# A quarter turn of an 8192 x 8192 matrix: six of eight output columns turned by VectorE and ScalarE instead of TensorE

## The chip, the core and the metric

The kernel runs on one core of a Trainium2 chip. The metric is the time of one execution in microseconds (us), as the device reports it, median of the runs; the launch on the host is not in it. A profiled execution of the same kernel gives the span from the first to the last instruction and the busy times of the engines: TensorE (PE for its products, PEld for its weight loads), VectorE (DVE), ScalarE (ACT), GpSimd (POOL) and SyncE (SP), and of the 16 DMA engines that move data between HBM and the on-chip memories SBUF and PSUM, both of 128 partitions.

## The reference

```python
def setup_inputs():
    return {"x": np.random.randn(8192, 8192).astype(np.float32), "k": 1}

def reference(x, k):
    return np.rot90(x, k)
```

With k = 1 element (r, c) of x goes to row 8191 - c, column r of the output: a transpose, with the columns of x taken from the last to the first. Nothing is computed; 268.4 MB are read and 268.4 MB written.

## The kernel before

**Tiling.** x is cut into 16 macro tiles of 1024 rows by 4096 columns (`macros`, index `kk`). A macro tile comes in as 8 loads (`t` = 0 to 7, T = 8) of 128 rows by 4096 columns, 2 MiB each, one row a partition; load number `m` is `kk * 8 + t`. It goes out as 8 outputs (`j` = 0 to 7, J = 8), each made of the 512 columns of one `j` over all 1024 rows: 512 output rows in 4 groups of 128 partitions, 1024 elements a row, 2 MiB. The last macro tile is put out otherwise: in two halves of 4 loads (END), two `j` at a time, in rows of 512 elements. One of its outputs is split in two (`n_few`): a quarter, put out with 64 partitions by 16 small stores from SyncE, and three quarters by one store.

**Buffers.** Five buffers of 2 MiB (`bufs`): in steady state two take loads (LAND) and three hold outputs (OUTS). Between them lies `ring`, 63 slots of 128 x 512 elements; slot numbers come from `slot(kk, t, j)`, and a macro tile's load `t` lands in the slots that output `t` of the macro tile before has left. So load m = n + 8 can be put into the ring only when output n has been read out of it.

**The work of the engines.** They run side by side, each through its own list in program order, and wait on semaphores.

- SyncE issues the loads (L178). From the sixth on each waits until VectorE has emptied the buffer (`s_rev`).
- VectorE (L238 to L256) waits for the load, waits for the slots, and copies the 8 x 512 columns into the ring with the order in each 512 reversed (L248). A load is cut into two or three pieces, by which slots are free first.
- TensorE (L268 to L293) turns 128 x 128 blocks: 32 transposes (L279) an output, 16 for each half of PSUM (`ps[0]`, `ps[1]`). Of output 0 of a macro tile the blocks of early loads are turned as they land.
- ScalarE (L299 to L331) waits for room in an out buffer (the store three outputs back), copies each half of PSUM into it (L317, 128 x 2048), and issues the store (L326).

`s_half` counts turned halves, `s_ev` evicted ones, `s_store` and `s_land` finished DMAs.

Of the kernel before, what the change touches and what calls it, by code (L numbers as in the profile page):

```python
# [6 lines left out]
P = 128  # L7
# [3 lines left out]
T = R // P  # L11
W = 4096
G = 4
J = W // (G * P)
# [3 lines left out]
CH = G * P  # L18
F = G * R
SLOTS = T * J - 1  # L20

END = T // 2

H = 2
LAND = 2
OUTS = 3

FEW = 16
LEFT = 4
# [23 lines left out]
def slot(kk, t, j):  # L53

    at = t * J + j if kk % 2 == 0 else J + t + j * T
    return (at + kk // 2 * (J + 1)) % SLOTS


def kernel(tc: tile.TileContext, x: bass.AP, k: bass.AP, out: bass.AP):
# [19 lines left out]
    n_few = n_out - J + 2  # L79
    kk, ts, js = outs[n_few]  # L80
    assert len(js) == 2 and END * P * H * G == F
    blocks = [(j, g * P, P) for j in reversed(js) for g in range(G)]
    few = [[(js[-1], g * P // 2 + h * FEW, P // 2) for g in range(G)] for h in range(H)]
    outs[n_few] = (kk, ts, js, few)
    outs.insert(n_few + 1, (kk, ts, js, [blocks[2 : 2 + G], blocks[2 + G :]]))
    n_out += 1

    def halves(n):
        if len(outs[n]) == 4:
            return outs[n][3]  # L90
        blocks = [(j, g * P, P) for j in reversed(outs[n][2]) for g in range(G)]
        return [blocks[: len(blocks) // H], blocks[len(blocks) // H :]]


    order = [(kk, a, b) for kk in range(KK) for a in range(T) for b in range(J)]
    for i, (kk, t, j) in enumerate(order):
        if i >= SLOTS:
            pk, pj, pt = order[i - SLOTS]
            assert slot(kk, t, j) == slot(pk, pt, pj)

    with tc.tile_critical():  # L101
# [9 lines left out]
        ]  # L111

# [4 lines left out]
        s_first = nc.alloc_semaphore("s_first")  # L117
        s_half = nc.alloc_semaphore("s_half")
        s_ev = nc.alloc_semaphore("s_ev")
        s_few = nc.alloc_semaphore("s_few")  # L120
# [14 lines left out]

        pieces, rev = {}, {}
        done = 0
        for m in range(n_load):  # L140
            kk, t = divmod(m, T)
            got = []
            if m >= T:
                full = (s_half, H * (m - T + 1))
                first = (s_first, m - T + 2)
            else:
                full = None
                first = (s_first, 1) if t == T - 1 else None
            begin = wide if kk == KK - 1 else 1
            cuts = [0, begin, J - 1, J] if t == T - 1 else [0, J - 1, J]  # L150
            if m < T - 1:
                cuts = [0, J]
            for lo, hi in zip(cuts[:-1], cuts[1:]):
                got.append((lo, hi, first if hi == J else full if lo == 0 else None))
                done += 1
                for j in range(lo, hi):
                    rev[m, j] = done
            pieces[m] = got

        def runs(kk, t, lo, hi):  # L160

            at = [slot(kk, t, j) for j in range(lo, hi)]
            i = 0
            while i < len(at):
                n = 1
                step = at[i + 1] - at[i] if i + 1 < len(at) else 1
                if step > 0:
                    while i + n < len(at) and at[i + n] - at[i + n - 1] == step:
                        n += 1
                else:  # L170
                    step = 1
                yield lo + i, n, at[i], step
                i += n
# [14 lines left out]
        with nc.Block() as block:  # L188
# [15 lines left out]
            @block.sync  # L204
            def _(e):
                for m in range(LAND + OUTS, n_load):
                    last = [i for i in range(m) if load_buf(i) == load_buf(m)]
                    e.wait_ge(s_rev, rev[last[-1], J - 1])
                    load(e, m)
                kk, ts, js, _ = outs[n_few]  # L210
                b = out_buf(n_few)
                top = M - macros[kk][1] - (js[-1] + 1) * CH
                left = macros[kk][0] + ts[0] * P
                rows = len(ts) * P
                for h in range(H):
# [14 lines left out]
                e.wait_ge(s_few, 16 * 2 * H * LEFT)  # L230
                for b in range(LAND + OUTS):
                    n = sum(out_buf(i) == b and i != n_few for i in range(n_out))
                    if n:
                        e.wait_ge(s_store[b], 16 * n)

            @block.vector
            def _(e):
                for m in range(n_load):  # L238
                    kk, t = divmod(m, T)
                    b = load_buf(m)  # L240
                    a = bufs[b][:].rearrange("p (j c) -> p j c", c=CH)
                    e.wait_ge(s_land[b], 16 * (uses_before(m, load_buf) + 1))
                    for lo, hi, wait in pieces[m]:
                        if wait:
                            e.wait_ge(*wait)
                        for j, n, at, step in runs(kk, t, lo, hi):
                            v = ring[:, at * CH : (at + (n - 1) * step + 1) * CH]
                            i = e.tensor_copy(  # L248
                                out=bass.AP(
                                    tensor=v.tensor,  # L250
                                    offset=v.offset,
                                    ap=[v.ap[0], [step * CH, n], [1, CH]],
                                ),
                                in_=a[:, j : j + n, ::-1],
                            )
                        i.then_inc(s_rev, 1)  # L256

            @block.tensor
            def _(e):
# [8 lines left out]
                for n, (kk, ts, js, *_) in enumerate(outs):  # L268
                    parts = halves(n)
                    rows = len(ts) * P  # L270

                    def transpose(t, h, b):
                        j, off, width = parts[h][b]
                        if n:
                            wait(s_ev, H * (n - 1) + h + 1)
                        wait(s_rev, rev[kk * T + t, j])
                        at = slot(kk, t, j) * CH + off
                        f = b * rows + (t - ts[0]) * P
                        i = e.transpose(  # L279
                            ps[h][:width, f : f + P], ring[:, at : at + width], ident  # L280
                        )
# [12 lines left out]

            @block.scalar
            def _(e):
                e.wait_ge(s_id, 2)
                e.copy(scratch, ident[:, :1])  # L298
                for n, (kk, ts, js, *_) in enumerate(outs):  # L299
                    r0, c0 = macros[kk]  # L300
                    parts = halves(n)
                    rows = len(ts) * P
                    b = out_buf(n)
                    for h in range(H):
                        if h == 0:
# [11 lines left out]
                        e.copy(  # L317
                            bufs[b][:width, h * F // H : h * F // H + f], ps[h][:width, :f]
                        ).then_inc(s_ev, 1)
                    if n == n_few:  # L320
                        continue
# [45 lines left out]
```

## Time and profile before

| | |
|---|---|
| median of 3 runs | 1264.5 us (1264.1 to 1264.59) |
| profiled execution, its own time | 1264.36 us |
| its span, first to last instruction | 1262.3 us |
| PE busy / PEld busy | 726.8 us (58%) / 683.2 us (54%), 4120 transposes |
| DVE busy | 403.0 us (32%), 313 instructions |
| ACT busy | 469.7 us (37%), 260 instructions |
| DMA | 537.48 MB, mean 426 GB/s |
| loads: 128 of 2048 KB | 16.8 us from issue to landing (median) |
| stores: 127 of 2048 KB, one of 1536 KB, 16 of 32 KB | 25.6 us for the large ones (median) |

Busy shares are of the span. The DMA row counts every byte that the engines moved, instructions included. The time from issue to landing holds the time that a transfer spends behind others in its queue.

### The profile page before, as it was taken

What the parts mean: (1) busy time and instruction counts of PE and PEld (TensorE: products, weight loads), DVE (VectorE), ACT (ScalarE), POOL (GpSimd) and SP (SyncE); (2) the same over time, 40 slices, a digit from 0 to 9 for tenths busy, and PEclk for the clock granted to TensorE, in tenths of its full rate; (3) what the DMA queues carried; (4) which work ended last, traced back from release to release, by engine and by line L of the source; (5) the groups of instructions that cost most, each with busy time, mean ns of one, the idle gap of its engine ahead of it and who ended that gap; (6) DMA issues with size and microseconds to landing.
All of it is one profiled execution on the core that took longest, in us unless ns stands there. A gap on an engine that the chain in (4) does not pass through costs nothing.

```text
span 1262.3 us, 9427 instructions
## 1 busy us (share of the span) xinstructions
PE 726.8 (58%) x4120; PEld 683.2 (54%) x4120; DVE 403.0 (32%) x313; ACT 469.7 (37%) x260; POOL 0.7 (0%) x6
## 2 busy tenths in 40 slices
PE   1566566665546645566555655566555655556564
PEld 1456465665545545565554655555555654556564
DVE  3323432324323343322342233422234222442210
ACT  0343333433334333433334333343333433434364
POOL 0000000000000000000000000000000000000000
PEclk9967767676787777777777776777777777777888
DMA  9999999999999999999999999999999999999998
GB/s 399 416 430 430 428 428 429 428 430 429 428 429 428 429 429 430 427 429 432 427 428 430 430 428 428 431 429 427 430 429 428 429 429 428 430 430 428 429 412 361
DMA packets 37032, 537.48 MB, mean 426 GB/s; under 512 B 4160, under 2 KB 4160, under 8 KB 4160
## 3 DMA queue, kind: packets, MB, share of 16 engines
q10 hardware_dynamic: 18432, 267.92, 50.0%
q1 hardware_dynamic: 18560, 268.97, 49.9%
q8 instruction: 32, 0.52, 0.2%
q14 instruction: 8, 0.07, 0.0%
HBM read 268.44 MB, written 268.44 MB: 425 GB/s over the span
## 4 chain that ended last, share of the span: by engine, by line
DMA 80%; issue 8%; DVE 5%; ACT 4%; PE 1%; SPq 1%; ACTq 0%
DMA buf<-in_x_dram 70%; DMA out_dram<-buf 11%; DVE ring L248 5%; ACT buf L317 4%; PE ps L279 1%; SPq L220 1%; ACTq L326 0%; SPq L178 0%; ACTq L314 0%; SPq L362 0%; SPq L101 0%
## 5 line engine op out<-in xcount | busy, mean ns | idle before, releaser
L279 PE MATMUL ps<-head,ring 128*128 128x128 f32 x4120 | 726.8, 357 | 522.7 <-ACT buf L317 462.3
L279 PEld LDWEIGHTS ps<-head,ring 128*128 128x128 f32 x4120 | 683.2, 190 | 566.1 <-ACT buf L317 497.2
L317 ACT COPY buf<-ps 128x2048 f32<-128x2048 f32 (+1 forms) x258 | 468.3, 1867 | 781.1 <-DMA out_dram<-buf 609.3
L248 DVE COPY ring<-buf 128x512 f32<-128x512 f32 (+7 forms) x313 | 403.0, 1337 | 811.4 <-DMA buf<-in_x_dram 810.1
L298 ACT ACT_TABLE_LOAD x1 | 1.3, 1283 | 0.9 <-SPq L101 0.9
L194 POOL TENSOR_SCALAR_AFFINE_SELECT head<-head 128x128 f32<-128x128 f32 x1 | 0.3, 292 | 0.2 <-POOL head L192 0.2
L192 POOL MEMSET head<- 128x128 f32 x1 | 0.2, 205 | 0.5 <-SPq L101 0.5
L298 ACT COPY head<-head 128x1 f32<-128x1 f32 x1 | 0.2, 191 | 0.0
L348 POOL MEMSET const-bfloat16-1.0<- 128x1 bf16 x1 | 0.1, 101 | 0.0
L348 POOL MEMSET const-uint8-127<- 128x1 uint8 x1 | 0.1, 101 | 0.0
L348 POOL MEMSET const-float32-0.0<- 128x1 f32 x1 | 0.1, 100 | 0.2 <-issue 0.2
L348 POOL MEMSET const-float32-1.0<- 128x1 f32 x1 | 0.1, 98 | 0.0
## 6 DMA issues: line engine op xcount, KB each, us to landing
buf<-in_x_dram SPq DMA_DIRECT2D x128, 2048.0 KB, 16.8
out_dram<-buf ACTq DMA_DIRECT2D x127, 2048.0 KB, 25.6
out_dram<-buf ACTq DMA_DIRECT2D x1, 1536.0 KB, 9.8
out_dram<-buf SPq DMA_DIRECT2D x16, 32.0 KB
```

The costliest lines, as they stand in the source:

```text
L192: e.memset(ident, 0.0).then_inc(s_id, 1)
L194: e.affine_select(out=ident, in_=ident, compare_op=mybir.AluOpType.not_equal, fill=1.0, base=0, pattern=[[-1, P]], channel_multiplier=1,). ...
L220: e.dma_start(out=bass.AP(tensor=out.tensor, offset=out[first : first + 1, left : left + 1].offset, ap=[[LEFT * M, FEW // LEFT], [4 * FEW ...
L248: i = e.tensor_copy(out=bass.AP(tensor=v.tensor, offset=v.offset, ap=[v.ap[0], [step * CH, n], [1, CH]],), in_=a[:, j : j + n, ::-1],)
L279: i = e.transpose(ps[h][:width, f : f + P], ring[:, at : at + width], ident)
L298: e.copy(scratch, ident[:, :1])
L317: e.copy(bufs[b][:width, h * F // H : h * F // H + f], ps[h][:width, :f]).then_inc(s_ev, 1)
L348: nc = _bacc.Bacc("TRN2", target_bir_lowering=False, num_devices=1)
```

## The change

The outputs of macro tiles 0 to 14 are divided (`in_quadrants`): `j` = 0 and 4 (BY_PE) are turned by TensorE as before, the other six by VectorE and ScalarE. For these six, VectorE puts the load's columns into the ring by 32 x 32 transposes (`e.transpose`, L289) in place of the reversing copy; 90 outputs in all. What is then left is to move whole 32 x 32 blocks from one group of 32 partitions to another (`moves`): 16 copies an output, each of 32 partitions by 8 x 4 x 32 elements, 8 of them by VectorE (L276) and 8 by ScalarE (L344), straight from the ring to the out buffer.

VectorE's list changes with it. Before it waits for load m = n + 8 it does its copies of output n, for which it waits for room in the out buffer (`room_for`) and for the macro tile's last load; and before it writes load m into the ring it waits for ScalarE's copies (`s_act`) and for its own (`s_dve`). ScalarE issues the store of such an output when both counts are there.

The ring becomes a fixed grid of 8 x 8 chunks, of which 63 lie in SBUF; the 64th, of load 7 and output 7, lies in the last 512 columns of PSUM (`corner`, in `ps[1]`). It makes 16 copies more for output 7, out of PSUM. So an output of TensorE is cut into three parts of 2048, 1536 and 512 columns (`parts`), the third in `ps[0]` again, and the last macro tile's transposes, which use all of PSUM, wait for all copies of the moved outputs (L306 to L308). A load is cut into two pieces (`j` 0 and 4, and the rest), load 7 of a macro tile into five. The last macro tile's outputs are 8 of 2 MiB; the split one and its 16 small stores go.

```diff
+Q = 32
+BY_DVE = 8
+BY_PE = [0, 4]
+
 END = T // 2
 
 H = 2
 LAND = 2
 OUTS = 3
-
-FEW = 16
-LEFT = 4
...
-    at = t * J + j if kk % 2 == 0 else J + t + j * T
-    return (at + kk // 2 * (J + 1)) % SLOTS
+    return t * J + j if kk % 2 == 0 else j * J + t
...
-    n_few = n_out - J + 2
-    kk, ts, js = outs[n_few]
-    assert len(js) == 2 and END * P * H * G == F
-    blocks = [(j, g * P, P) for j in reversed(js) for g in range(G)]
-    few = [[(js[-1], g * P // 2 + h * FEW, P // 2) for g in range(G)] for h in range(H)]
-    outs[n_few] = (kk, ts, js, few)
-    outs.insert(n_few + 1, (kk, ts, js, [blocks[2 : 2 + G], blocks[2 + G :]]))
-    n_out += 1
...
+    outs = [(*o, [(j, g * P) for j in reversed(o[2]) for g in range(G)]) for o in outs]
+    def in_quadrants(kk, j):
+        return kk < KK - 1 and j not in BY_PE
+
+    moved = [in_quadrants(kk, js[0]) for kk, _, js, _ in outs]
+
+
+    parts, seen = {}, 0
+    for n, (kk, ts, js, blocks) in enumerate(outs):
+        if moved[n]:
+            continue
+        end = len(blocks) * len(ts) * P
+        ends = [F // H, F - CH, F] if kk < KK - 1 else [F // H, end]
+        parts[n] = []
+        for i, (lo, hi) in enumerate(zip([0, *ends], ends)):
+            parts[n].append((seen, i % H, lo, hi))
+            seen += 1
+
+    def moved_until(n):
+        return sum(moved[: n + 1])
...
+        corner = ps[1][:, F // H - CH :]
...
+        def room_for(e, n):
+            b = out_buf(n)
+            stores = [i for i in range(n) if out_buf(i) == b]
+            loads = [i for i in range(n_load) if load_buf(i) == b]
+            if stores:
+                e.wait_ge(s_store[b], 16 * len(stores))
+            elif loads:
+                e.wait_ge(s_rev, rev[loads[-1], J - 1])
...
+            by_pe = list(range(J)) if kk == KK - 1 else BY_PE
+            rest = [j for j in range(J) if j not in by_pe]
+            if t < T - 1:
+                got = [js for js in (by_pe, rest) if js]
             else:
-                full = None
-                first = (s_first, 1) if t == T - 1 else None
-            begin = wide if kk == KK - 1 else 1
-            cuts = [0, begin, J - 1, J] if t == T - 1 else [0, J - 1, J]
-            if m < T - 1:
-                cuts = [0, J]
-            for lo, hi in zip(cuts[:-1], cuts[1:]):
-                got.append((lo, hi, first if hi == J else full if lo == 0 else None))
+                if kk == KK - 1:
+                    got = [by_pe[:wide], by_pe[wide:-1], by_pe[-1:]]
+                else:
+                    got = [by_pe[:1], *neighbours(rest[:-1]), by_pe[1:], rest[-1:]]
+            assert sorted(j for js in got for j in js) == list(range(J))
...
+        def moves(n, share):
+            kk, ts, (j,), _ = outs[n]
+            rows = len(ts) * P
+            cut = T - 1 if j == J - 1 else T
+            s, ((step, _),) = spaced([slot(kk, t, j) for t in ts[:cut]])
+            for lo, hi, v, first in ((0, cut, ring[:], s * CH), (cut, T, corner, 0)):
+                for a, q in share if lo < hi else []:
+                    yield (
+                        at(
+                            bufs[out_buf(n)][q * Q : q * Q + Q, :],
+                            lo * P + a * Q,
+                            [[P, hi - lo], [rows, G], [1, Q]],
+                        ),
+                        at(
+                            v[a * Q : a * Q + Q, :],
+                            first + q * Q,
+                            [[step * CH, hi - lo], [P, G], [1, Q]],
+                        ),
+                    )
+
+        pairs = [(a, q) for a in range(P // Q) for q in range(P // Q)]
...
-                kk, ts, js, _ = outs[n_few]
-                b = out_buf(n_few)
-                top = M - macros[kk][1] - (js[-1] + 1) * CH
-                left = macros[kk][0] + ts[0] * P
-                rows = len(ts) * P
-                for h in range(H):
-                    e.wait_ge(s_ev, H * n_few + h + 1)
-                    for at in (0, 2 * FEW):
-                        for d in range(LEFT):
-                            first = top + h * FEW + at + d
-                            e.dma_start(
-                                out=bass.AP(
-                                    tensor=out.tensor,
-                                    offset=out[first : first + 1, left : left + 1].offset,
-                                    ap=[[LEFT * M, FEW // LEFT], [4 * FEW * M, G], [1, rows]],
-                                ),
-                                in_=bufs[b][
-                                    at + d : at + FEW : LEFT, h * F // H : (h + 1) * F // H
-                                ].rearrange("m (g f) -> m g f", f=rows),
-                            ).then_inc(s_few, 16)
-                e.wait_ge(s_few, 16 * 2 * H * LEFT)
                 for b in range(LAND + OUTS):
...
                 for m in range(n_load):
                     kk, t = divmod(m, T)
                     b = load_buf(m)
-                    a = bufs[b][:].rearrange("p (j c) -> p j c", c=CH)
+                    n = m - T
+                    if n >= 0 and moved[n]:
+                        room_for(e, n)
+                        e.wait_ge(s_rev, rev[n // J * T + T - 1, n % J])
+                        for to, of in moves(n, pairs[:BY_DVE]):
+                            i = e.tensor_copy(out=to, in_=of)
+                        i.then_inc(s_dve, 1)
                     e.wait_ge(s_land[b], 16 * (uses_before(m, load_buf) + 1))
-                    for lo, hi, wait in pieces[m]:
-                        if wait:
-                            e.wait_ge(*wait)
-                        for j, n, at, step in runs(kk, t, lo, hi):
-                            v = ring[:, at * CH : (at + (n - 1) * step + 1) * CH]
-                            i = e.tensor_copy(
-                                out=bass.AP(
-                                    tensor=v.tensor,
-                                    offset=v.offset,
-                                    ap=[v.ap[0], [step * CH, n], [1, CH]],
-                                ),
-                                in_=a[:, j : j + n, ::-1],
-                            )
-                        i.then_inc(s_rev, 1)
+                    if n >= 0:
+                        if moved[n]:
+                            e.wait_ge(s_dve, moved_until(n))
+                            e.wait_ge(s_act, moved_until(n))
+                        else:
+                            e.wait_ge(s_half, turned_until(n))
+                    for js in pieces[m]:
+                        if (m, js[0]) == (n_load - 1, J - 1):
+                            e.wait_ge(s_half, turned_until(KK * J - J))
+                        turn = e.transpose if in_quadrants(kk, js[0]) else e.tensor_copy
+                        turn(out=chunk(kk, t, js), in_=landed(b, js)).then_inc(s_rev, 1)
 
             @block.tensor
             def _(e):
@@ -265,64 +298,61 @@
                         e.wait_ge(sem, n)
 
                 e.wait_ge(s_id, 2)
-                for n, (kk, ts, js, *_) in enumerate(outs):
-                    parts = halves(n)
+                used = {}
+                for n, (kk, ts, js, blocks) in enumerate(outs):
+                    if moved[n]:
+                        continue
                     rows = len(ts) * P
-
-                    def transpose(t, h, b):
-                        j, off, width = parts[h][b]
-                        if n:
-                            wait(s_ev, H * (n - 1) + h + 1)
+                    if n == KK * J - J:
+                        wait(s_act, moved_until(n))
+                        wait(s_dve, moved_until(n))
+                    order = [
+                        (part, f) for part in parts[n] for f in range(part[2], part[3], P)
+                    ]
+                    if js[0] == 0 and kk < KK - 1:
+                        late = parts[n][-1]
+                        order.sort(key=lambda o: (o[0] == late, o[1] % rows, o[1]))
+                    last = dict(order)
+                    for part, f in order:
+                        _, h, lo, _ = part
+                        j, off = blocks[f // rows]
+                        t = ts[f % rows // P]
+                        if used.get(h, part) != part:
+                            wait(s_ev, used[h][0] + 1)
                         wait(s_rev, rev[kk * T + t, j])
-                        at = slot(kk, t, j) * CH + off
-                        f = b * rows + (t - ts[0]) * P
                         i = e.transpose(
-                            ps[h][:width, f : f + P], ring[:, at : at + width], ident
+                            ps[h][:, f - lo : f - lo + P],
+                            chunk(kk, t, [j])[:, 0, off : off + P],
+                            ident,
                         )
-                        if t == ts[-1] and b == len(parts[h]) - 1:
+                        if f == last[part]:
                             i.then_inc(s_half, 1)
-                        elif t == ts[0] and h == H - 1 and b == len(parts[h]) - 1:
-                            i.then_inc(s_first, 1)
-
-                    order = [
-                        (t, h, b) for h in range(H) for b in range(len(parts[h])) for t in ts
-                    ]
-                    if js[0] == 0:
-                        order.sort()
-                    for t, h, b in order:
-                        transpose(t, h, b)
+                            used[h] = part
 
             @block.scalar
             def _(e):
                 e.wait_ge(s_id, 2)
                 e.copy(scratch, ident[:, :1])
-                for n, (kk, ts, js, *_) in enumerate(outs):
+                for n, (kk, ts, js, blocks) in enumerate(outs):
                     r0, c0 = macros[kk]
-                    parts = halves(n)
                     rows = len(ts) * P
                     b = out_buf(n)
-                    for h in range(H):
-                        if h == 0:
-                            stores = [i for i in range(n) if out_buf(i) == b]
-                            loads = [i for i in range(n_load) if load_buf(i) == b]
-                            if stores and stores[-1] == n_few:
-                                e.wait_ge(s_few, 16 * 2 * H * LEFT)
-                            elif stores:
-                                e.wait_ge(s_store[b], 16 * sum(i != n_few for i in stores))
-                            elif loads:
-                                e.wait_ge(s_rev, rev[loads[-1], J - 1])
-                        e.wait_ge(s_half, H * n + h + 1)
-                        width = parts[h][0][2]
-                        f = len(parts[h]) * rows
-                        e.copy(
-                            bufs[b][:width, h * F // H : h * F // H + f], ps[h][:width, :f]
-                        ).then_inc(s_ev, 1)
-                    if n == n_few:
-                        continue
-                    groups = sum(len(part) for part in parts)
+                    room_for(e, n)
+                    if moved[n]:
+                        e.wait_ge(s_rev, rev[kk * T + T - 1, js[0]])
+                        for to, of in moves(n, pairs[BY_DVE:]):
+                            i = e.copy(to, of)
+                        i.then_inc(s_act, 1)
+                        e.wait_ge(s_act, moved_until(n))
+                        e.wait_ge(s_dve, moved_until(n))
+                    else:
+                        for k, h, lo, hi in parts[n]:
+                            e.wait_ge(s_half, k + 1)
+                            e.copy(bufs[b][:, lo:hi], ps[h][:, : hi - lo]).then_inc(s_ev, 1)
+                        e.wait_ge(s_ev, turned_until(n))
+                    groups = len(blocks)
                     top = M - c0 - js[0] * CH - groups * P
                     left = r0 + ts[0] * P
-                    e.wait_ge(s_ev, H * (n + 1))
                     e.dma_start(
                         out=out[top : top + groups * P, left : left + rows].rearrange(
                             "(g m) f -> m g f", m=P

```

More of the change, by code (lines that the diff above doesn't have):

```diff
@@ L78, with turned_until @@
     assert len(outs) == n_out
-    n_few = n_out - J + 2
-    kk, ts, js = outs[n_few]
-    assert len(js) == 2 and END * P * H * G == F
-    blocks = [(j, g * P, P) for j in reversed(js) for g in range(G)]
-    few = [[(js[-1], g * P // 2 + h * FEW, P // 2) for g in range(G)] for h in range(H)]
-    outs[n_few] = (kk, ts, js, few)
-    outs.insert(n_few + 1, (kk, ts, js, [blocks[2 : 2 + G], blocks[2 + G :]]))
-    n_out += 1
[L88 to L99, printed above, removed]
+    outs = [(*o, [(j, g * P) for j in reversed(o[2]) for g in range(G)]) for o in outs]
[14 more added lines that the diff above has]
+        return sum(moved[: n + 1])
+    def turned_until(n):
+        return sum(len(parts[i]) for i in range(n + 1) if i in parts)
     with tc.tile_critical():
@@ L116 @@
         s_rev = nc.alloc_semaphore("s_rev")
-        s_first = nc.alloc_semaphore("s_first")
         s_half = nc.alloc_semaphore("s_half")
         s_ev = nc.alloc_semaphore("s_ev")
-        s_few = nc.alloc_semaphore("s_few")
+        s_dve = nc.alloc_semaphore("s_dve")
+        s_act = nc.alloc_semaphore("s_act")
         def load_buf(m):
@@ L134, in out_buf, with neighbours @@
             return ends[e % len(ends)]
+        def room_for(e, n):
[6 more added lines that the diff above has]
+                e.wait_ge(s_rev, rev[loads[-1], J - 1])
+        def neighbours(js):
+            cuts = [i for i in range(1, len(js)) if js[i] != js[i - 1] + 1]
+            return [js[lo:hi] for lo, hi in zip([0, *cuts], [*cuts, len(js)])]
         pieces, rev = {}, {}
@@ L141 @@
             kk, t = divmod(m, T)
[L142 to L145, printed above, removed]
-            else:
-                full = None
-                first = (s_first, 1) if t == T - 1 else None
-            begin = wide if kk == KK - 1 else 1
-            cuts = [0, begin, J - 1, J] if t == T - 1 else [0, J - 1, J]
-            if m < T - 1:
-                cuts = [0, J]
-            for lo, hi in zip(cuts[:-1], cuts[1:]):
-                got.append((lo, hi, first if hi == J else full if lo == 0 else None))
+            by_pe = list(range(J)) if kk == KK - 1 else BY_PE
@@ new lines @@
+            rest = [j for j in range(J) if j not in by_pe]
+            if t < T - 1:
+                got = [js for js in (by_pe, rest) if js]
+            else:
+                if kk == KK - 1:
[3 more added lines that the diff above has]
+            assert sorted(j for js in got for j in js) == list(range(J))
+            pieces[m] = got
+            for js in got:
@@ L155, with spaced @@
                 done += 1
-                for j in range(lo, hi):
+                for j in js:
                     rev[m, j] = done
[L158 to L173, printed above, removed]
+        def spaced(js):
+            step = js[1] - js[0] if len(js) > 1 else 1
+            n = 1
+            while n < len(js) and js[n] - js[n - 1] == step:
+                n += 1
+            if n == len(js):
+                return js[0], [[step, n]]
+            far = js[n] - js[0]
+            assert js == [js[0] + i * far + s * step for i in range(len(js) // n) for s in range(n)]
+            return js[0], [[far, len(js) // n], [step, n]]
@@ new lines, in at, with landed, chunk @@
+        def at(v, first, dims):
+            return bass.AP(
+                tensor=v.tensor, offset=v[:, first : first + 1].offset, ap=[v.ap[0], *dims]
+            )
+        def landed(b, js):
+            j, dims = spaced(js)
+            return at(
+                bufs[b][:], (j + 1) * CH - 1, [*([s * CH, n] for s, n in dims), [-1, CH]]
+            )
+        def chunk(kk, t, js):
+            if (t, js[0]) == (T - 1, J - 1):
+                if kk < KK - 1:
+                    return at(corner, 0, [[CH, 1], [1, CH]])
+                return at(ring[:], 0, [[CH, 1], [1, CH]])
+            s, dims = spaced([slot(kk, t, j) for j in js])
+            assert max(slot(kk, t, j) for j in js) < SLOTS
+            return at(ring[:], s * CH, [*([d * CH, n] for d, n in dims), [1, CH]])
@@ new lines, in moves @@
+        def moves(n, share):
[16 more added lines that the diff above has]
+                        ),
+                    )
@@ L209, in _ @@
                     load(e, m)
-                kk, ts, js, _ = outs[n_few]
-                b = out_buf(n_few)
-                top = M - macros[kk][1] - (js[-1] + 1) * CH
-                left = macros[kk][0] + ts[0] * P
-                rows = len(ts) * P
-                for h in range(H):
-                    e.wait_ge(s_ev, H * n_few + h + 1)
-                    for at in (0, 2 * FEW):
-                        for d in range(LEFT):
-                            first = top + h * FEW + at + d
-                            e.dma_start(
-                                out=bass.AP(
-                                    tensor=out.tensor,
-                                    offset=out[first : first + 1, left : left + 1].offset,
-                                    ap=[[LEFT * M, FEW // LEFT], [4 * FEW * M, G], [1, rows]],
-                                ),
-                                in_=bufs[b][
-                                    at + d : at + FEW : LEFT, h * F // H : (h + 1) * F // H
-                                ].rearrange("m (g f) -> m g f", f=rows),
-                            ).then_inc(s_few, 16)
-                e.wait_ge(s_few, 16 * 2 * H * LEFT)
                 for b in range(LAND + OUTS):
-                    n = sum(out_buf(i) == b and i != n_few for i in range(n_out))
+                    n = sum(out_buf(i) == b for i in range(n_out))
                     if n:
```

## The prediction

> **What bounds the kernel now.** I read the page's slices first, then the waits, the timeline of two steps in mid-kernel, the groups by form, and the windows of the tail.
>
> ```profile
> DMA  9999999999999999999999999999999999999998
> GB/s 399 416 430 430 428 428 429 428 430 429 428 429 428 429 429 430 427 429 432 427 428 430 430 428 428 431 429 427 430 429 428 429 429 428 430 430 428 429 412 361
> ```
>
> The 16 DMA engines are full in every slice, at 427 to 432 GB/s between the first two slices and the last two. 268.4 MB in and 268.4 MB out at 429 GB/s are 1251 us of the 1262.3 us span. The rest is about 11 us at both ends; no compute edit can win more than a part of it.
>
> ```profile
> DVE ring L248 <- DMA buf<-in_x_dram: 810.1, 128, 8.5
> ACT buf L317 <- DMA out_dram<-buf: 609.3, 104, 7.0
> ```
>
> Waits: engine, awaited, total us, times, longest. VectorE waits for loads, ScalarE for stores to give a buffer back. Both are spare time.
>
> ```profile
> 524.27 3.63 ACT L317 COPY buf<-ps 128x2048 f32<-128x2048 f32 x2 [6.11 <-DMA out_dram<-buf]
> 525.02 2.69 DVE L248 COPY ring<-buf 128x2048 f32<-128x2048 f32 x3 [7.33 <-DMA buf<-in_x_dram]
> ...
> 534.03 3.63 ACT L317 COPY buf<-ps 128x2048 f32<-128x2048 f32 x2 [6.13 <-DMA out_dram<-buf]
> 534.74 2.69 DVE L248 COPY ring<-buf 128x2048 f32<-128x2048 f32 x3 [7.03 <-DMA buf<-in_x_dram]
> ```
>
> Timeline: start, us, engine. One output and one load every 9.76 us, which is 2 x 2.097 MB at 429 GB/s. ScalarE works 3.63 us plus 0.55 us of issue (L326) of it, VectorE 2.69 us. The budget of the change is therefore 9.76 us per step, 78.1 us per macro tile of eight steps.
>
> **The change, part by part.** The bytes, the order of loads and stores and the buffers (two to land, three out) stay. What moves is who rearranges, and how long a buffer is held. The rows that price it:
>
> ```profile
> L317 ACT COPY buf<-ps 128x2048 f32<-128x2048 f32 x255 | 463.7, 1870 | 780.5 <-DMA out_dram<-buf 609.3 <-PE ps L279 167.3 <-DVE ring L248 3.8
> ...
> L248 DVE COPY ring<-buf 128x3072 f32<-128x3072 f32 x24 | 42.1, 1755 | 49.5 <-DMA buf<-in_x_dram 49.5
> ...
> L248 DVE COPY ring<-buf 128x1024 f32<-128x1024 f32 x17 | 11.7, 687 | 55.7 <-DMA buf<-in_x_dram 55.7
> ...
> L317 ACT COPY buf<-ps 128x1024 f32<-128x1024 f32 x1 | 1.0, 1018 | 0.0
> ```
>
> ```profile
> 593.27 3.89 DVE L248 COPY ring<-buf 128x3584 f32<-128x3584 f32 x1 [7.27 <-DMA buf<-in_x_dram]
> ```
>
> VectorE thus shows two speeds: 1755 ns for 3072 elements a partition (and 687 for 1024) is 0.52 ns an element plus 0.15 us; 3.89 us for 3584 is 1.04 ns plus 0.15 us. Two or three in a row overlap by 0.08 us each (1.22 + 1.22 + 0.41 against 2.69 above).
>
> *The load's step (L289).* One copy of 2 x 512 at 0.69 us, then one transpose of 3072 elements. No transpose is in the trace. Bounds: 1.76 us (fast rate) and twice the slow rate, 6.54 us. I take the slow rate itself, 3.34 us: the middle of the three, and a pace that this engine shows. Step: 0.69 + 3.34 - 0.08 = 3.95 us. [...]
>
> *The copies of a moved output.* Eight on VectorE (L276) and eight on ScalarE (L344), each 32 partitions by 1024 elements in runs of 32. No 32-partition copy is in the trace. VectorE: 0.61 us (fast, with the 0.08 us of overlap that the rows show between full-width copies) to 1.21 us (slow). I take 0.69, the 1024-element row, and no overlap, because each copy goes to other partitions than the one before, which no two copies of the trace do: 8 x 0.69 = 5.5 us, against 4.9 with the overlap. [...] ScalarE: 1018 ns for 1024 elements out of PSUM, 0.1 us of overlap (2 x 1.87 against 3.63): 8 x 1.02 - 0.7 = 7.5 us; it reads SBUF now, so 7.0 to 9.5, I take 7.7. With 0.55 issue and 0.2 of semaphores, 8.5 us.
>
> *Column 7* takes 7/8 of that (8 x 0.62 = 5.0 on VectorE) plus eight small copies out of the corner in PSUM, 0.2 to 0.4 us each by ScalarE's 191 ns for one column and the 414 ns of 512: 2.3 us. Load 7 of a macro tile is split in five: 0.41 + 1.75 + 1.21 + 0.41 + 0.68 - 0.32 = 4.1 us.
>
> *VectorE's sum over a macro tile:* two PE columns 2 x 3.95, five moved steps 5 x (5.5 + 3.95), column 7 at 5.0 + 2.3 + 4.1 = 11.4 us: 66.6 us, with 0.15 us of semaphores a step 67.8 us against 78.1. *ScalarE:* 5 x 8.5 + (8.5 + 1.3) + 2 x 4.7 = 61.7 us. Both fit. TensorE's 4120 transposes fall to 1216; since DMA releases everything, that is worth 0.
>
> *Where the wait goes.* In L270 to L289 VectorE first waits for room (the store three back), copies, waits for the load, then for ScalarE's half (`s_act`), then transposes; queued behind that wait are the landing buffer's release and SP's next load (L259). ScalarE's store waits for VectorE's half (`s_dve`). A landing buffer comes round every 19.5 us: 9.76 at half rate, about 2.3 of latency (the first load: issued 0.96, landed 8.19, less 4.9 of bytes), 3.95 of work; 3.5 us may be waited. In columns 5 to 7 VectorE is late by 2 x (9.6 - 9.76) + (11.55 - 9.76) = about 1.5 us: covered, and column 0, which has no VectorE copies, makes it up. An out buffer has 29.3 - 9.76 - 2.3 - 8.5 = 8.7 us to spare. So the DMA engines stay fed in mid-kernel: 0.
>
> *Start:* output 1 can begin only when load 8 has left its buffer (47.1 + 3.95 = 51.1 us), and takes 7.7 us: stored at 59 instead of 54.7 us. Store 0 and loads 9 and 10 keep DMA busy to about 61 us (6.3 MB from 46.2). Thin cover, 0 to 2 us lost; I take 0.8.
>
> *End:*
>
> ```profile
> 1210.00:1220.00 10.00, 8.06 (x68) 7.16 (x66) 2.50 (x4) 8.65 (x5) 0.00 (x0) 0.98 0.96 405
> 1220.00:1230.00 10.00, 7.23 (x60) 6.48 (x60) 0.00 (x0) 8.46 (x6) 0.00 (x0) 1.00 0.96 401
> ```
>
> Windows, last column GB/s: the tail is stores alone at about 401. Two things change. The split output's 16 small stores (L220) go: 0.5 MB is 1.3 us of the queue, and how it lay on the 16 engines is not shown; -1.3 to +1.3, I take +0.6, that it evened them out. And TensorE may begin the last macro tile only after column 7's copies (L307), 16 transposes at 1.98 us, two evictions and an issue, 6.3 us to the next store; about 1.2 stores and output 119 (11 us) cover it; 0 to 2, I take 0.7.
>
> *Sum:* 1264.36 (profiled execution: span 1262.3 and 2.06 around it) + 0.8 + 0.6 + 0.7 = 1266.5 us. The median of the three runs before is 1264.5, 0.1 above the profiled one, so it stands for the median too.
>
> **The rivals.**
>
> *A. VectorE becomes the bound.* If the 32-partition copies run at the slow rate, a moved step is 8 x 1.21 + 3.95 = 13.6 us and column 7 8.6 + 2.3 + 4.1 = 15.0: 7.9 + 68 + 15 + 1.2 = 92.1 us a macro tile, 14 over 78.1; over 15 of them 210 us: 1475. A transpose of 6.54 us makes the load's step 7.15, column 7 5.0 + 2.3 + 7.3 = 14.6: 2 x 7.15 + 5 x 12.65 + 14.6 + 1.2 = 93.4, 1494. It decides from 78.1 us a macro tile. For it: runs of 32, and L248's odd shapes do fall to the slow rate here. Against: the strided form of seven blocks ran 3584 elements in 2.29 us at 1202.05, so gaps do not slow it, and 8 and 7 blocks stand alike on both sides of each copy.
>
> *B. The buffers turn too slowly though the averages fit.* Gaps between eight dependent copies, 10.5 us a moved step and 13 in column 7, make VectorE 4.7 us late against 3.5: 1.2 us, or up to 3 with gaps between the transposes too, of idle DMA per macro tile, 15 times: 18 to 45 us, 1284 to 1311. ScalarE at 1.2 us a copy would do the same. For it: 3.5 us is small. Against: when loads run dry, stores still fill the 16 engines.
>
> *C. As forecast, but start and end at their upper bounds:* 0.8 + 0.6 + 0.7 become 2 + 1.3 + 2: 1269.7.
>
> *D. Faster:* the small stores cost more than they evened out (-1.3), the two evictions that go with the split (1.86 us each) bring the last stores forward by 1.5, and nothing is lost at the start: 1264.36 - 2.8 = 1261.6.
>
> **Chances.** About 0.2% (2.5 us) is what a measurement of this kernel can tell from no change. Forecast 0.37, A 0.15, B 0.22, C 0.16, D 0.10. Faster is D, 0.10; same is the forecast, 0.37; slower is A, B and C, 0.53. The range leaves out A: 1261 to 1310. Most of the chance lies on slower, spread over three mechanisms, while the likeliest single case is the forecast; its own range is 1262 to 1267.
>
> **What would show it.** Right: L276 near 0.69 us, the transpose near 3.4, VectorE busy about 1015 us (15 x 66.6, and 8 x 2.3 for the last macro tile's loads), and all middle slices at 427 to 432 GB/s; VectorE still waiting for loads at columns 0 and 4. A: L276 at 1.2 us or the transpose over 6, GB/s near 365 and no waits on DMA. B: the right durations, but GB/s at 415 to 425 in the middle and SP waiting for VectorE with loads dry. C or D: a middle unchanged, and the first two and last two slices other than 399, 416, 412 and 361. The prediction is wrong if the middle slices lose more than 1% or the transposes' pace is not 1.04 ns an element.

## The result, and the profile after

| | before | after |
|---|---|---|
| median | 1264.3 us (1264.07 to 1264.59, 4 runs) | 1284.18 us (1283.06 to 1284.52, 4 runs) |
| ratio to before | 1 | 1.0156, 95% interval 1.0138 to 1.0173 |
| span of the profiled execution | 1262.3 us | 1282.5 us |
| DVE / ACT busy | 403.0 / 469.7 us | 1036.9 / 909.6 us |

The kernel is 1.6% slower. It lies inside the range, and not where the likeliest case stood (1266.5): 18 us above it, at the lower end of rival B. The slices show where the time went:

```profile
DMA  9999999999999999999999999999999999999988
GB/s 398 418 420 424 429 431 399 429 428 430 430 394 429 430 428 430 395 431 427 431 429 384 429 429 432 426 408 428 431 427 431 395 428 430 432 413 410 431 362 368
```

Most middle slices stand at 427 to 432 GB/s as before. But about every fifth falls to 384 to 413: slices 7, 12, 17, 22, 27, 32 and 36 with 37. Five slices of 32.06 us are 160 us, two macro tiles. So something fails in every *second* macro tile. The distance of each slice from 429 GB/s, times its length, adds up to the time that DMA lost:

| us lost against 429 GB/s | slices 1 to 4 | 5 to 38 | 39 and 40 | sum |
|---|---|---|---|---|
| before | 3.0 | 0.4 | 6.3 | 9.6 |
| after | 4.2 | 16.6 | 9.6 | 30.3 |

Of the growth, 16.2 us come from the middle, 3.3 from the end and 1.2 from the start; that is 20.7 us, where the span grew by 20.2. (The differences are taken before rounding.) The middle's 16.6 us are 1.5% of its 1090 us, so by the sign that the prediction set itself ("wrong if the middle slices lose more than 1%") its forecast did not hold.

The groups by form (one row for each shape: count, then busy us and mean ns) are those that the prediction had to bound:

```profile
L344 ACT COPY buf<-ring 32x1024 f32<-32x1024 f32 x600 | 624.9, 1042 | 191.0 <-DVE buf L276 148.4 <-DMA out_dram<-buf 13.1 <-DVE ring L289 11.2
L276 DVE COPY buf<-ring 32x1024 f32<-32x1024 f32 x600 | 407.0, 678 | 7.3
L289 DVE STREAM_TRANSPOSE ring<-buf 128x3072 f32<-128x3072 f32 x105 | 354.0, 3371 | 0.0
...
L276 DVE COPY buf<-ring 32x896 f32<-32x896 f32 x120 | 103.3, 861 | 1.4
```

The 32-partition copy (678 ns against 0.69 us) and the transpose (3371 against 3.34 us) came out as priced. The last row did not: 896 elements took longer than 1024. Its mean mixes two speeds, which VectorE's timeline shows in two neighbouring macro tiles, 5 and 6:

```profile
506.29 8.66 DVE L276 COPY buf<-ring 32x896 f32<-32x896 f32 x8
514.97 2.35 DVE L276 COPY buf<-ps 32x128 f32<-32x128 f32 x8
...
586.49 5.50 DVE L276 COPY buf<-ring 32x896 f32<-32x896 f32 x8
592.01 2.36 DVE L276 COPY buf<-ps 32x128 f32<-32x128 f32 x8
```

Column 7's eight copies take 8.66 us in the odd macro tile, 5.50 us in the even one. Behind the first DMA runs short, behind the second it does not (windows; the last two columns are DMA share and GB/s):

```profile
510.00:520.00 10.00, 0.90 (x3) 0.50 (x3) 9.75 (x16) 3.72 (x10) 0.00 (x0) 0.50 0.94 398
520.00:530.00 10.00, 7.29 (x32) 6.55 (x32) 9.70 (x12) 9.26 (x10) 0.00 (x0) 0.58 0.98 354
590.00:600.00 10.00, 2.55 (x10) 1.75 (x11) 8.41 (x16) 6.57 (x12) 0.00 (x0) 0.50 1.00 428
```

Loads and stores were both late there: no store was issued between 502.13 and 517.41 us and no load between 506.39 and 521.62, 15 us each, where the budget has one of each every 9.76.

And the waits have turned around:

```profile
DVE ring L289 <- DMA buf<-in_x_dram: 177.9, 94, 8.4
ACT buf L344 <- DVE buf L276: 171.7, 50, 6.7
...
ACT buf L344 <- DMA out_dram<-buf: 13.1, 13, 2.9
```

VectorE's 810 us of waiting for loads are down to 178; ScalarE, which waited 609 us for stores, now waits 172 for VectorE and hardly for stores. There is spare time left on the mean, but little of it at any one place.

**Theory 1.** Column 7 of the odd macro tiles runs at VectorE's slow rate (8 x (896 x 1.04 ns + 0.15 us) is 8.65 us, against 8.66 measured). There the slots of a column lie side by side (`j * J + t`), so the source's 7 chunks of 4 blocks (32 elements every 128 columns) can be read as one run of 28 blocks, while the destination stays 7 by 4; in even ones the chunks lie 8 slots apart, and both sides are 7 by 4. Seven such columns would make some 15 of the 20 us. **Theory 2.** The buffers turn too slowly in general (rival B as written), and the dips come with column 7 because it is the longest. **The end:** TensorE's late start in the last macro tile.

### The profile page after: what moved, and what is told of

The parts are those of the page before. It is cut to its first block, busy times and chain, and to the rows that moved or that the text cites. A ratio compares the mean times of both kernels' runs of the same rounds, so it can differ in the third digit from the quotient of the medians.

```text
span 1282.5 us, 5292 instructions
## 1 busy us (share of the span) xinstructions
PE 254.2 (20%) x1216; PEld 207.1 (16%) x1216; DVE 1036.9 (81%) x1135; ACT 909.6 (71%) x948; POOL 0.7 (0%) x6
## 5 line engine op out<-in xcount | busy, mean ns | idle before, releaser
L344 ACT COPY buf<-ring 32x1024 f32<-32x1024 f32 x720 | 737.1, 1024 | 217.1 <-DVE buf L276 171.7
L276 DVE COPY buf<-ring 32x1024 f32<-32x1024 f32 x720 | 510.3, 709 | 8.7
L323 PE MATMUL ps<-head,ring 128*128 128x128 f32 x1216 | 254.2, 382 | 1011.2 <-DVE ring L289 493.8
L289 DVE STREAM_TRANSPOSE ring<-buf 128x3072 f32<-128x3072 f32 x135 | 397.5, 2953 | 0.0
L323 PEld LDWEIGHTS ps<-head,ring 128*128 128x128 f32 x1216 | 207.1, 200 | 1058.1 <-DVE ring L289 508.0
L289 DVE COPY ring<-buf 128x1024 f32<-128x1024 f32 (+2 forms) x145 | 103.9, 717 | 188.9 <-DMA buf<-in_x_dram 177.9
L351 ACT COPY buf<-ps 128x2048 f32<-128x2048 f32 (+2 forms) x106 | 140.1, 1391 | 138.7 <-PE ps L323 119.0
L276 DVE COPY buf<-ps 32x128 f32<-32x128 f32 x120 | 33.9, 282 | 1.7
L344 ACT COPY buf<-ps 32x128 f32<-32x128 f32 x120 | 31.0, 258 | 1.4
L289 DVE STREAM_TRANSPOSE ps<-buf 128x512 f32<-128x512 f32 x15 | 10.7, 717 | 0.0
```

The source lines that it names most:

```text
L276: i = e.tensor_copy(out=to, in_=of)
L289: turn(out=chunk(kk, t, js), in_=landed(b, js)).then_inc(s_rev, 1)
L323: i = e.transpose(ps[h][:, f - lo : f - lo + P], chunk(kk, t, [j])[:, 0, off : off + P], ident,)
L344: i = e.copy(to, of)
L351: e.copy(bufs[b][:, lo:hi], ps[h][:, : hi - lo]).then_inc(s_ev, 1)
```

## The experiments

All were timed beside the kernel before (1264.5 to 1264.7 us in those runs).

**Exchange of two dimensions.** In `moves`, for all copies:

```diff
-                            [[P, hi - lo], [rows, G], [1, Q]],
+                            [[rows, G], [P, hi - lo], [1, Q]],
...
-                            [[step * CH, hi - lo], [P, G], [1, Q]],
+                            [[P, G], [step * CH, hi - lo], [1, Q]],
```

> The two outer dimensions of the 32-partition copies are exchanged (groups outside, chunks inside), so that 4 stands outermost on both sides whatever the slots are. Theory 1 (the slow column 7 of the odd macro tiles makes the dips): the 32x896 copies take 0.62 to 0.69 us in every macro tile, column 7 of the odd ones falls from 8.66 to about 5.2 us on VectorE, the slices near 395 GB/s go, and the time falls by 7 x 2.3 = 16 us to about 1268 us. Theory 2 (the buffers turn too slowly in general, because VectorE, ScalarE and the two landing buffers wait for each other): the copies get faster but dips stay at each column 7; less than 3 us gained, 1281 us or more.

Measured: 1271.57 us, ratio 1.0059 (1.0046 to 1.0071), 12.6 us less than the changed kernel. By form, in the timeline of macro tile 5, and in slices:

```profile
L276 DVE COPY buf<-ring 32x896 f32<-32x896 f32 x120 | 73.5, 612 | 1.4
```

```profile
502.07 4.99 DVE L276 COPY buf<-ring 32x896 f32<-32x896 f32 x8
...
507.07 2.36 DVE L276 COPY buf<-ps 32x128 f32<-32x128 f32 x8
```

```profile
GB/s 397 415 428 422 429 430 429 429 429 429 429 428 430 428 430 430 429 430 425 429 429 417 429 429 430 429 423 428 417 430 430 428 429 421 429 427 419 430 370 364
```

The dips to 395 are gone, the middle's loss falls from 16.6 to 3.6 us, and nothing but the order in which VectorE and ScalarE walk the same elements was changed (ScalarE's copies took 1041 and 935 ns, as before). Theory 1 holds. It was too high by some 3 us (16 expected): some dips of 417 to 423 remain. That the chunks lie side by side does not slow a copy by itself: in macro tile 5 of the changed kernel the columns of eight such chunks took 5.52 us each, as in macro tile 6.

**The even ones made slow too.** VectorE's copies of column 7 in even macro tiles, cut in four:

```diff
-            for lo, hi, v, first in ((0, cut, ring[:], s * CH), (cut, T, corner, 0)):
+            ranges = [(0, cut, ring[:], s * CH)]
+            if j == J - 1 and kk % 2 == 0 and share[0] == (0, 0):
+                ranges = [(lo, min(lo + 2, cut), ring[:], (s + lo * step) * CH) for lo in range(0, cut, 2)]
+            for lo, hi, v, first in [*ranges, (cut, T, corner, 0)]:
```

> VectorE's copies of column 7 are cut in four (2, 2, 2 and 1 chunks) in the even macro tiles, which ran at the fast rate so far: some 3 us more for each, as much as the odd ones lose already. Theory 1: dips of some 2.3 us come to the seven or eight even macro tiles as well, time up by 7 x 2.3 to 8 x 2.5, 1300 to 1304 us. Theory 2: the extra 3 us are taken up by the 10 us of VectorE's spare time in a macro tile; up by less than 5 us, below 1289.

Measured: 1299.93 us, ratio 1.0276 (1.0262 to 1.0291), 15.8 us more, the lower end of Theory 1. By the groups (192 pieces of 282 ns and 64 of 217 in place of 64 copies of 677) VectorE worked 3.1 us more in each of eight columns, and each cost 2.0 us of time. The row of 32x896 now holds the odd macro tiles alone, and shows their rate unmixed:

```profile
L279 DVE COPY buf<-ring 32x896 f32<-32x896 f32 x56 | 60.0, 1071 | 0.7
```

Its slices:

```profile
GB/s 396 420 424 393 415 431 403 431 406 424 430 409 431 384 427 431 401 429 399 431 431 406 428 401 430 429 403 429 398 431 430 403 429 396 431 422 418 428 332 366
```

Dips now come at every second or third slice, that is in every macro tile, and the middle loses 27.3 us. So most of a lateness at column 7 is paid at once, although VectorE has some 10 us of idle time in the same macro tile. Theory 2's "taken up by spare time" fails here, as its "dips stay" failed above.

**An earlier start for TensorE.** The wait of L306 to L308, asked only for the half of PSUM with the corner:

```diff
-                    if n == KK * J - J:
-                        wait(s_act, moved_until(n))
-                        wait(s_dve, moved_until(n))
...
+                        if n == KK * J - J and h == H - 1:
+                            wait(s_act, moved_until(n))
+                            wait(s_dve, moved_until(n))
```

> TensorE's wait for all copies of the moved outputs, ahead of the last macro tile, is asked only before transposes into the half of PSUM that holds the corner; the other half may be filled as loads land. Theory: of the last macro tile's start 3.7 us (16 transposes at the low granted clock, 1229.2 to 1232.97) leave the path, store 120 is issued near 1234 instead of 1237.65 us, and the DMA dip at 1232 to 1242 us (283 GB/s) shrinks: 2 to 3.5 us gained, 1281 to 1282 us. Rival: the dip comes from column 7 of macro tile 14 alone, and the time stays within 1 us of 1284.2.

Measured: 1280.58 us, ratio 1.0128 (1.0114 to 1.0141), 3.6 us less. In the changed kernel's timeline the wait stands in front of everything:

```profile
1229.22 0.55 ACTq L356 DMA_DIRECT2D out_dram<-buf  x1
...
1229.23 8.23 PE L323 MATMUL ps<-head,ring 128*128 128x128 f32 x48 [37.72 <-DVE buf L276]
1232.97 1.87 ACT L351 COPY buf<-ps 128x2048 f32<-128x2048 f32 x1 [5.52 <-PE ps L323]
...
1237.65 0.55 ACTq L356 DMA_DIRECT2D out_dram<-buf  x1
```

8.4 us pass between two stores, while one takes some 5 us at 401 GB/s; DMA falls to 283 GB/s from 1232 to 1242 us. With the edit ScalarE begins its first eviction at 1228.66 us, the store goes at 1233.66, and the same window has 395 GB/s. The theory holds, with a gain just above its 2 to 3.5 us; the end's loss falls from 9.6 to 6.6 us.

**The kernel before without its split output.** In the kernel before, the split and SyncE's 16 small stores are taken out, nothing else:

```diff
-    n_few = n_out - J + 2
...
-    outs[n_few] = (kk, ts, js, few)
-    outs.insert(n_few + 1, (kk, ts, js, [blocks[2 : 2 + G], blocks[2 + G :]]))
-    n_out += 1
+    n_few = -1
...
-                e.wait_ge(s_few, 16 * 2 * H * LEFT)
```

> The kernel before without its split output: the last macro tile is put out in eight stores of 2 MiB, no small stores from SyncE, one output and two evictions fewer. The prediction's term: +0.6 us, within -1.3 and +1.3, so 1264.9 us. Rival: the split evens out the 16 engines' ends by more, 2 us or more.

Measured: 1265.39 us against 1264.66, ratio 1.0005 (0.9996 to 1.0014). The term's 0.6 us is what it looks like, though the interval takes in zero.

**Both edits together.**

> The exchange of the two dimensions and TensorE's earlier start together. Theory: the two losses lie apart, so their gains add: 1271.6 - 3.6 = 1268.0 us, still some 3 us above the kernel before (0.7 of it the unsplit output, the rest small dips at the odd column 7 and the last macro tile's late first stores). Rival: with faster column 7 copies TensorE's start is no longer late, so at most 1 us is added: 1270.5 us or more.

Measured: 1269.06 us, ratio 1.0037 (1.0025 to 1.005). The second edit adds 2.5 us, between theory and rival. With the exchange alone the two stores around the wait were already 7.4 us apart (1216.77 and 1224.16) instead of 8.4; that less was therefore left to gain is the likely reason, not a shown one.

**Halved copies in the other five columns.** VectorE's copies of columns 1, 2, 3, 5 and 6, two of 4 chunks each in place of one of 8 (the rest of the edit puts the two halves of a copy next to each other):

```diff
...
+            if j < J - 1 and share[0] == (0, 0):
+                ranges = [(lo, lo + 4, ring[:], (s + lo * step) * CH) for lo in (0, 4)]
...
```

> VectorE's copies of columns 1, 2, 3, 5 and 6 are each cut in two halves of 4 chunks (512 elements) that read from and write to the same groups of 32 partitions, one right after the other. Theory of the change of quadrant: a half takes 0.41 us, and the second of each two overlaps the first by 0.08 us as full-width copies do, so 16 halves take 8 x (0.42 + 0.34) = 6.1 us. Rival: 32-partition copies never overlap, 16 x 0.42 = 6.7 us. Either way VectorE has 0.6 to 1.2 us more in each of five columns, so the time goes up by 15 x 5 x 0.6 to 1.2 us x some 0.6 = 27 to 54 us if every us of VectorE's counts, or by under 15 us if only what is late at column 7 counts.

Measured: 1289.48 us, ratio 1.0202 (1.0186 to 1.0218), 5.3 us more than the changed kernel. VectorE's timeline:

```profile
540.49 6.07 DVE L280 COPY buf<-ring 32x512 f32<-32x512 f32 x16
```

A half is 411 ns busy; sixteen without overlap would be 6.6 us. They take 6.07: 0.5 us of overlap, 0.06 for each two with the same partitions on both sides, against the theory's 0.08. Where each copy changes the quadrant there is none (eight of 678 ns in 5.52 us). That it is the second of each two that overlaps is inferred from the sums. The time is the other lesson: 0.55 us more in each of five columns, 15 times, is 41 us of VectorE's work, and cost 5.3, the second of the two cases expected (under 15 us).

**Seven to nine.** Both edits, and in those five columns VectorE does 7 copies, ScalarE 9:

```diff
+        def by_dve(n):
+            return BY_DVE - (n % J < J - 1)
...
```

> As both edits together, but in columns 1, 2, 3, 5 and 6 VectorE does 7 of the 16 copies and ScalarE 9: VectorE's moved step falls by 0.69 us to 9.0, ScalarE's rises by 1.04 to 10.0 us, over the 9.76 us of a step, though its mean over a macro tile (about 72 us) still fits. Theory that VectorE's lateness is the whole loss: the dips left go, 1265 to 1267 us. Rival: ScalarE becomes the late one, VectorE waits for its count before it may write the ring, dips grow, 1270 us or more.

Measured: 1269.54 us, ratio 1.004 (1.0028 to 1.0053): the same as without. VectorE's busy time fell from 1007.2 to 955.7 us for nothing. Neither theory is right as put: the time did not fall, nor did it rise to 1270, and ScalarE, busy 987.8 us, became no bound either. By the slices the middle lost 0.7 us less than with both edits alone (2.9 after 3.6), and the start 1.3 us more (5.2 after 3.8). So most of what is left is not VectorE's time in these five columns.

**Column 7 without the corner.** Both edits, and the 32x128 copies left out, so that this version leaves part of the output unwritten:

```diff
...
-            for lo, hi, v, first in ((0, cut, ring[:], s * CH), (cut, T, corner, 0)):
+            for lo, hi, v, first in ((0, cut, ring[:], s * CH),):
```

> As both edits together, with the sixteen 32x128 copies out of the corner in PSUM left out of each column 7, so the last 128 output columns of these outputs' macro tile rows are not written from it. VectorE loses 2.4 and ScalarE 2.2 us of column 7. Theory (what is left above the kernel before is still lateness at column 7, on both engines): the slices at 417 to 424 GB/s in mid-kernel rise to 429, and the last moved output comes 2.4 us sooner: 3 to 4 us gained on 1269.1, 1265 to 1266 us. Rival (what is left lies at the start and in the last macro tile's stores): 1 to 2 us gained at most, 1267 us or more.

Measured: 1266.97 us, ratio 1.0019 (1.001 to 1.0028), 2.1 us less. The middle's loss falls from 3.6 to 1.5 us. That is between the two: the corner's copies are worth 2 us. Of the 2.4 us still above the kernel before, 0.7 is the missing split; by the slices the start loses 1.0, the middle 1.2 and the end, the split with it, 1.0 us more than before. That rest was not taken apart by an experiment.

## Why the prediction was right and wrong

- **What bounds the kernel, and the budget.** Right. DMA at 429 GB/s sets every slice where it is fed, and losses of time are losses of DMA feed.
- **Transpose and 32-partition copy.** Right, 3.37 and 0.68 us; eight in 5.52 us against 5.5. The transpose's pace was chosen as the middle of three bounds, so that it came out is in part luck. That copies to other partitions do not overlap was the author's assumption; no row of before showed it. The runs then showed eight of 678 ns in 5.52 us where the quadrant changes, and sixteen halves of 411 ns in 6.07 us, not 6.58, where it changes only with every second one.
- **ScalarE's copies.** Eight take 8.41 us, not 7.7; the term was 0.7 us too small. In mid-kernel VectorE never waited for them; it did once, for 3.0 us, at the start, behind output 1.
- **Column 7: the step that failed.** "Column 7 takes 7/8 of that (8 x 0.62 = 5.0 on VectorE)" holds in no macro tile: 5.50 us in the even, 8.66 in the odd ones. Rival A's sentence "8 and 7 blocks stand alike on both sides of each copy" is where it was lost. I read the shapes as the code writes them, not as they look once adjacent dimensions are one. The trace of before had shown the penalty, 3.89 us against 2.29 for the same 3584 elements, where seven adjacent chunks are one run on one side:

```profile
L248 DVE COPY ring<-buf 128x3584 f32<-128x3584 f32 x63 | 212.9, 3380 | 390.8 <-DMA buf<-in_x_dram 390.8
```

By `slot`, 43 of these 63 copies go to adjacent slots and 20 to slots 8 apart; 43 x 3.89 + 20 x 2.29 is 213.1 us, the row's busy time within 0.2. Six chunks took 1755 ns in the mean of 24 copies, though 10 of them went to adjacent slots. In the runs 28 against 7 took 1071 ns, 7 against 7 676 and 4 against 4 612. That the source is folded to 28 blocks is inferred from the layout and from the exchange's success; no view prints the folded shape.
- **Column 7 in the even macro tiles.** There the "7/8" failed too, by half a us, for another reason: seven blocks on both sides take as long as eight. A copy of 896 elements took 676 ns where 1024 took 678, and only with 4 outermost did it fall to 612. The kernel before shows the same, with eight blocks of 512 in the first row and seven in the second:

```profile
L248 DVE COPY ring<-buf 128x4096 f32<-128x4096 f32 x7 | 16.1, 2294 | 23.6 <-DMA buf<-in_x_dram 23.6
```

```profile
1202.05 2.29 DVE L248 COPY ring<-buf 128x3584 f32<-128x3584 f32 x1 [7.20 <-DMA buf<-in_x_dram]
```

At the prediction's own 0.52 ns an element plus 0.15 us the seven blocks would take 2.01 us. They take the 2.29 us of eight, so the row that rival A quotes as free of a penalty carries a small one.
- **What may be late.** The numbers left 2.0 us of spare at column 7 (3.5 allowed, 1.5 used). With 3.7 us more than assumed, 1.7 us of lateness follow in each of the seven odd macro tiles, 12 us in all; the exchange gained 12.6, though it also made column 7 of the even ones half a us faster. So the landing buffer's sum gives the size of the loss. It was still too generous: in the exchange's run column 7 was as priced (4.99 + 2.36 us against 5.0 + 2.3) and should have cost nothing, yet the middle lost 3.6 us, and leaving out the corner's copies (2.4 us on VectorE, 2.2 on ScalarE) brought 2.1 us back. It also follows the loads alone, while in the slow column both loads and stores were late; no run separates the two. It is a limit at one place: 3.1 us at column 7 cost 2.0, while 2.7 us spread over five columns cost 0.35 a macro tile.
- **Rival B** had the right place and price (1284 to 1311) and the wrong cause, gaps between copies. There are none: 8 x 0.678 is 5.42 of 5.52 us. The cause was A's slow rate, in 7 of 90 outputs. What B had against it, that stores still fill the 16 engines when loads run dry, did not hold (398 and 354 GB/s). That the time met B's price is in part luck: seven stalls of some 2 us and 3.3 us at the end add up to about what fifteen of 1.2 us would.
- **Start.** 0.8 us; the first four slices lost 1.2 more.
- **End.** The split's term of +0.6 measured 0.7, with zero inside the interval. TensorE's late start, put at 0.7 and within 2, was worth 3.6 by itself and 2.5 beside the exchange. The sum was short because the 16 transposes took 3.7 us (1229.23 to 1232.97), not 1.98, and because output 119 did not cover them: its store came 12.1 us after the one before it (1217.09 and 1229.22), and DMA stood at 371 GB/s already from 1222 to 1232 us.

## What to carry to other kernels

VectorE's copy of the same 896 elements took 1071 ns with seven chunks side by side in the source, 676 ns with them 8 slots apart, and 612 ns with the four groups outermost on both sides; that the merging of adjacent dimensions is the cause is inferred, as said above. So look up a copy's time in each layout that a loop goes through, and where one is slower, try another order of the dimensions. A mean that fits its budget is not enough; sum the longest stretch between two releases of a buffer and compare it with what that buffer may wait. When losses come with a period, convert the period into loop steps first: "every second macro tile" pointed at the cause before any experiment did. None of the versions tried beats the kernel before, because it was DMA-bound already and only its start and end could give.

## What the runs showed of the hardware that was not expected

- Seven blocks outermost on both sides cost VectorE as much as eight (676 against 678 ns, 2.29 against 2.294 us); with four outermost the same seven took 612 ns.
- ScalarE's 32-partition copies out of SBUF do not overlap one another either: 8 x 1.042 is 8.34 of 8.41 us, where two 128-partition evictions of 1.87 us take 3.63.
- TensorE, busy 20% instead of 58%, was granted less: 0.57 instead of 0.77 in the mean and 0.50 in most slices. After 37.7 us of rest, at a granted 0.50, its first 16 transposes took 3.7 us, still at 0.50; from 1237.67 us 16 took 1.97 us at 1.00, and before, 16 took 1.98 us in the tail, at 1.00. The prediction took that row of a busy tail for a start after a rest. That the clock alone makes the difference is not shown: at the start of the kernel before, four took 1.11 us (at 30.00) and later 0.65 us (at 505.74), with 1.00 recorded at both.
- VectorE's transposes, which read their source backwards, ran at the pace of its slow copies: 3072 elements in 3.37 us, 1.05 ns each with 0.15 us fixed, where the reversing copy of as many took 1.755 us. Whether a transpose that reads forwards is faster, no run shows.
